# A hybrid diffusion step: late transposition in the retention, an out projection for two chunks at a time, and a paced sparse mixer

## The chip, the cores and the metric

The kernel runs on one core of a Trainium2 chip. The metric is the time of one execution on the device, in microseconds (us), as the median of several runs. The engines are TensorE (PE in the rows, and PEld for its weight loads), VectorE (DVE), ScalarE (ACT), GpSimd (POOL) and SyncE (SP), which here only issues DMA transfers. Each engine works through its own list of instructions strictly in order, so an instruction that waits holds up all that stand behind it on that engine.

## What is computed

One inference step of a two-layer trunk for two groups of tokens: a prompt of 128 tokens and a sample of 512 latent tokens, both of width 1024. Layer 0 mixes tokens by a bidirectional retention, layer 1 by windowed attention; each layer ends with a channel mixer that picks 128 of 16,384 single-neuron experts for every token (PEER). Cut to what matters here:

```python
# retention (layer 0), per head h (4 heads, key width 256, value width 512)
o  = retention(q, k, v)                     # (tokens, 512), both directions
o  = (o - mean(o)) * rsqrt(var(o) + eps)    # per token and head
y  = (silu(g) * o) @ w_out                  # 4 heads * 512 -> 1024
x  = layer_norm(alpha * x + gate * y)
# PEER (after each mixer), per token
s  = (x @ wq) . keys;  top 16 by 16, then the best 16 of each of 8 heads -> e, w
a  = gelu(sum(u[e] * x));  x = layer_norm(alpha * x + gate * sum((w * a) * v[e]))
```

## The kernel before

Tokens go in chunks of 128: one chunk of the prompt and four of the sample. PEER is done in two ways. Sample chunks 1 to 3 of each layer go the dense way (`dense`): all experts are multiplied, and a weight table of zeros and selected weights, which `scatter` makes on VectorE, GpSimd, ScalarE and TensorE (L884 to L897) and writes to device memory, masks them. The prompt and sample chunk 0 go the sparse way (`sparse`): for each of 128 slots one indirect DMA on GpSimd's queue (L817) gathers 128 rows of 2048 numbers into one of five row buffers, VectorE forms a dot product (L821), and adds the weighted second half to `acc` (L809). Two slots form a group.

In layer 0 the sample's retention runs head by head. `ret_project` makes q, k, v and the gate of a head, with matrix products of 512 columns (L325) and of 256 (L348). `ret_whole` takes a head's four chunks in turn: `pairs` makes the scores of the chunk after this one (L424) and VectorE weighs them (`att`, L427); L443 and L447 add up the chunk's output `po`; then `ret_finish` takes its mean and variance (L363, L365), multiplies by the gate into `y` (L367), starts the reciprocal root on VectorE (L178 to L180), goes on with it on ScalarE, which also scales an identity by it (`diag`, L369), and multiplies `y` by `diag` on TensorE (L372), which scales and transposes in one step; ScalarE copies the result into `yT`. `mix` interleaves one head's `ret_whole` with the projection of the next head by a fixed ratio of steps; the last head has no projection beside it.

After the retention come, per sample chunk, the out projection (`out_proj`, L228, with weights in sixteen blocks of 512 KB from device memory for each call), the layer norm (L201 to L206), the scores (L653, L658), the top-16 search on VectorE (L628 to L636) and the selection (L692 to L775, transposed by TensorE at L780). The prompt's layer-1 attention (from L495) also stands in this stage; it starts from `xp1`, the prompt after its sparse PEER of layer 0. The stage ends with the last `scatter`, and `dense` (L864) of layer 0 follows.

Program order is only a priority: a scheduler at build time puts each engine's instructions in order, and work written later is taken early where it fits. So the prompt's sparse PEER, written behind the retention (`go(sparse(0, 0, ...))`), stands in VectorE's list among the retention's own steps.

## Time and profile before

| quantity | value |
|---|---|
| median of 3 runs | 4226.44 us |
| lowest and highest run | 4223.5 and 4227.94 us |
| the profiled execution, whole | 4227.91 us |
| its span from first to last instruction | 4225.8 us |
| mean granted clock of TensorE over the span | 0.965 |

The profiled execution lies 1.5 us above the median. 2.1 us of it lie outside the span.

### The profile page before, as it was taken

The page shows a single profiled execution, that of the slowest core. Times are in us where ns is not written, and L with a number is a line of the kernel's source. Part 1 is how long each engine was busy: PE and PEld are TensorE (multiplying, and loading weights), DVE is VectorE, ACT ScalarE, POOL GpSimd, SP SyncE. Part 2 cuts the span into 40 slices and gives each one's busy share as a digit, 9 for nine tenths or more (in the row PEclk, how much of TensorE's full clock was granted, in tenths as well). Part 3 has the DMA queues.
Part 4 walks back from the last instruction along what each step waited for, and adds up shares of the span by engine and source line. Part 5 has one row for each costly group of instructions (what it writes and reads, how often), then busy time and mean ns, then how long its engine had stood idle before and what let it go on. Part 6 is the DMA issues. An engine that isn't in the chain of part 4 may idle for free.

```text
span 4225.8 us, 57107 instructions
## 1 busy us (share of the span) xinstructions
PE 3928.4 (93%) x20292; PEld 3265.7 (77%) x20292; DVE 3154.8 (75%) x6873; ACT 1675.1 (40%) x3934; POOL 1139.7 (27%) x902
## 2 busy tenths in 40 slices
PE   7998989689987999999999979899879999999996
PEld 4675666456977999999999956577669999999995
DVE  1128888825877898888898933666678989888899
ACT  2212232211664444444444433455534444444442
POOL 0002333200673222222222300334422222222232
PEclk8999999899998999999999989999989999999998
DMA  9978888788876898988888725457689889898885
GB/s 375 366 240 326 333 334 319 273 261 276 268 233 207 304 362 325 350 334 336 331 343 336 294 83 157 137 165 220 181 297 346 327 339 340 336 352 328 333 339 218
DMA packets 485453, 1227.84 MB, mean 291 GB/s; under 512 B 27568, under 2 KB 302640, under 8 KB 409392
## 3 DMA queue, kind: packets, MB, share of 16 engines
q1 hardware_dynamic: 411440, 687.30, 47.5%
q0 software_dynamic: 73728, 536.90, 32.7%
q8 instruction: 159, 2.61, 0.2%
q14 instruction: 126, 1.03, 0.1%
HBM read 1166.69 MB, written 57.41 MB: 290 GB/s over the span
## 4 chain that ended last, share of the span: by engine, by line
PE 50%; issue 7%; DVE 4%; DMA 3%; POOL 3%; ACT 1%; SPq 0%; POOLq 0%; DVEq 0%; ACTq 0%
PE bank L864 20%; PE acc L864 19%; POOL rows L817 3%; PE aside L653 2%; PE bank L495 2%; PE sc L894 2%; DMA rows<-keysT 1%; PE aside L228 1%; PE bank L609 1%; PE bank L591 1%; DMA v<-uv 1%; DMA wh<-attn_w_in 1%; DMA wo<-attn_w_out 0%; DMA rows<-uv,ei 0%; PE sc L609 0%
## 5 line engine op out<-in xcount | busy, mean ns | idle before, releaser
L817 POOL DMA_INDIRECT rows<-uv,ei x512 | 767.5, 1499 | 2235.6 <-DVE acc L809 1639.8
L864 PE MATMUL bank<-hH,uH 128*128 128x384 f32 x2048 | 697.1, 340 | 26.2 <-ACT uH L856 22.1
L864 PE MATMUL bank<-hH,uL 128*128 128x384 f32 x2048 | 696.5, 340 | 6.3 <-DVE uL L857 6.3
L864 PE MATMUL bank<-hL,uH 128*128 128x384 f32 x2048 | 696.5, 340 | 0.0
L821 DVE CUSTOM_DVE_ANT_0 rows<-rows,h 128x1024 f32<-128x1024 f32 x512 | 623.8, 1219 | 63.0 <-DMA rows<-uv,ei 62.6
L809 DVE SCALAR_TENSOR_TENSOR acc<-rows,co,acc 128x1024 f32<-128x1024 f32 x508 | 651.1, 1282 | 7.2
L864 PE MATMUL acc<-vH,cH 128*128 128x512 f32 x1536 | 599.4, 390 | 4.0 <-ACT cH L856 4.0
L864 PE MATMUL acc<-vL,cH 128*128 128x512 f32 x1536 | 598.9, 390 | 0.0
L864 PE MATMUL acc<-vH,cL 128*128 128x512 f32 x1536 | 528.2, 389 | 0.0
L856 ACT CAST uH<-u 128x1024 fp32r<-128x1024 f32 x256 | 269.6, 1053 | 582.7 <-PE bank L864 560.5
L857 DVE TENSOR_TENSOR uL<-u,uH 128x1024 fp32r<-128x1024 f32 x256 | 313.1, 1223 | 141.2 <-ACT uH L856 130.5
L864 PEld LDWEIGHTS bank<-hH,uH 128*128 128x128 f32 x2048 | 386.8, 189 | 37.2 <-ACT uH L856 22.7
L864 PEld LDWEIGHTS bank<-hL,uH 128*128 128x128 f32 x2048 | 386.5, 189 | 9.7
L864 PEld LDWEIGHTS bank<-hH,uL 128*128 128x128 f32 x2048 | 386.3, 189 | 7.6 <-DVE uL L857 7.6
L856 ACT CAST vH<-v 128x1024 fp32r<-128x1024 f32 x256 | 268.9, 1051 | 247.3 <-PE acc L864 235.3
L857 DVE TENSOR_TENSOR vL<-v,vH 128x1024 fp32r<-128x1024 f32 x256 | 312.8, 1222 | 66.9 <-ACT vH L856 65.9
L864 PEld LDWEIGHTS acc<-vH,cL 128*128 128x128 f32 x1536 | 288.3, 188 | 59.9
L864 PEld LDWEIGHTS acc<-vH,cH 128*128 128x128 f32 x1536 | 288.9, 188 | 54.9 <-ACT cH L856 4.7
L864 PEld LDWEIGHTS acc<-vL,cH 128*128 128x128 f32 x1536 | 288.9, 188 | 50.0
L348 PE MATMUL bank<-w,hT 128*128 128x256 f32 x1280 | 295.8, 389 | 26.1 <-DVE vg L353 14.6
L348 PEld LDWEIGHTS bank<-w,hT 128*128 128x128 f32 x1280 | 246.5, 195 | 80.3 <-DVE vg L353 17.1
L890 POOL TENSOR_SCALAR rows<-cst,sel 128x128 f32<-128x128 f32 x192 | 176.8, 930 | 479.3 <-ACT sel L781 324.8
(391 smaller groups left out, 5865.3 us busy)
## 6 DMA issues: line engine op xcount, KB each, us to landing
u<-ut SPq DMA_DIRECT2D x256, 512.0 KB, 7.6
v<-uv SPq DMA_DIRECT2D x256, 512.0 KB, 7.0
wh<-wq SPq DMA_DIRECT2D x160, 512.0 KB, 5.7
w<-ret_w_in SPq DMA_DIRECT2D x48, 1024.0 KB, 9.1
Wd<-stg SPq DMA_DIRECT2D x48, 1024.0 KB, 6.1
W<-Wd SPq DMA_DIRECT2D x32, 1536.0 KB, 11.5
yT<-mod_w SPq DMA_DIRECT2D x40, 1024.0 KB, 10.1
wo<-ret_w_out SPq DMA_DIRECT2D x80, 512.0 KB, 5.9
```

Of the source, the lines that this page charges most:

```text
L228: PE.matmul(acc[j], aTs[j][:, kk, :], w[:, k, :], start=(kk == 0), stop=(kk == nk - 1))
L348: PE.matmul(p[:, :256], st.hT[:, k, c * P:(c + 1) * P], w[:, k, :], start=(k == 0), stop=(k == KT - 1))
L495: PE.matmul(p[:, :256], hT[:, k, :], w[k], start=(k == 0), stop=(k == KT - 1))
L653: PE.matmul(p[:, :T], w[k][:, a * P:(a + 1) * P], hT[:, k, :], start=(k == 0), stop=(k == KT - 1))
L809: V.scalar_tensor_tensor(acc, rows[j][:, D:], co[:, j:j + 1], acc, op0=ALU.mult, op1=ALU.add)
L817: G.indirect_dma_start(out=r, out_offset=None, in_=uv[i], in_offset=bass.IndirectOffsetOnAxis(ap=ei[:, sl:sl + 1], axis=0))
L821: V.tensor_tensor_reduce(rows[j][:, :D], rows[j][:, :D], h2, 1.0, 0.0, ALU.mult, ALU.add, a[:, j:j + 1])
L856: S.copy(hi, x)
L857: splits.append(V.tensor_tensor(lo, x, hi.bitcast(F32), op=ALU.subtract))
L864: PE.matmul(out, x, y, start=start and n == 0, stop=stop and n == 2, skip_group_check=True)
L890: (G if t > 1 else V).tensor_scalar(ah[:, t, :], C["iota"], sel[:, 0, t0 + t:t0 + t + 1], sel[:, 2, t0 + t:t0 + t + 1], op0=ALU.is_equal, ...
L894: PE.matmul(p[:, t * P:(t + 1) * P], ah[:, t, :], bh[:, t, :], start=True, stop=True)
```

## The change

It has three parts.

1. `ret_finish` is split. `ret_norm` does the statistics, `y` and `diag`; `ret_turn` does the product with `diag` and the copy. In `ret_whole` a chunk's `ret_turn` now comes after the next chunk's L443 and L447. For that `y` takes a slot of `att`'s ring, which has three buffers in place of two, and `diag` has two.
2. `out` takes two chunks for one pass over the out projection's weights: first chunks 1 and 2, then chunks 3 and 0 beside the scores of chunk 1. The scores of chunks 2, 3 and 0 then all run beside the prompt's attention and the scatters; before, those of chunk 2 ran beside the fourth out projection.
3. `sparse` of the prompt in layer 0 is paced. `ret_norm` records each of its VectorE steps that make `y`. Groups 0 to 2 are free; from group 3 on, two or three groups at a time are traced within `issue_after` of the next recorded step of the sample's 16, so that their VectorE instructions stand behind it in VectorE's list; groups 40 to 63 stand behind the sixteenth.

```diff
@@ -241,6 +241,8 @@
 
 
     hident = const.tile([P, P], F32, name="hident")
+
+    paced = []
 
     def ret_consts(rc, tmp):
         V.tensor_scalar(hident, ident, 0.5, None, op0=ALU.mult)
@@ -358,15 +360,19 @@
         for st, out in zip(streams, got):
             st.heads.append((h, *out))
 
-    def ret_finish(rp, h, c, po, sg, yT):
+    def ret_norm(rp, c, po, sg, deep=1):
+
         bn = lnp.tile([P, 6], F32, name="gbn")
         V.bn_stats(bn, po)
         mv = lnp.tile([P, 2], F32, name="gmv")
         V.bn_aggr(mv, bn)
-        y = rp.tile([P, 512], F32, name="y")
-        V.scalar_tensor_tensor(y, po, mv[:, 0:1], sg[:, c, :], op0=ALU.subtract, op1=ALU.mult)
-        diag = rp.tile([P, P], F32, name="diag")
+        y = rp.tile([P, 512], F32, name="y", tag="att" if deep > 1 else "y", bufs=3 if deep > 1 else 1)
+        paced.append(V.scalar_tensor_tensor(y, po, mv[:, 0:1], sg[:, c, :], op0=ALU.subtract, op1=ALU.mult))
+        diag = rp.tile([P, P], F32, name="diag", bufs=deep)
         S.activation(diag, hident, AF.Identity, scale=rstd_of(mv[:, 1:2], scalar=True))
+        return y, diag
+
+    def ret_turn(h, c, y, diag, yT):
         p = bank()
         for j in range(4):
             PE.matmul(p[:, j * P:(j + 1) * P], y[:, j * P:(j + 1) * P], diag, start=True, stop=True)
@@ -396,7 +402,7 @@
         V.tensor_tensor(att, pa[:, :P], M[:, h, :], op=ALU.mult)
         PE.matmul(po, att, v[:, 0, :], start=True, stop=True, skip_group_check=True)
         yield
-        ret_finish(rp, h, 0, po, sg, yT)
+        ret_turn(h, 0, *ret_norm(rp, 0, po, sg), yT)
 
     def ret_whole(rp, rc, stream, yT):
 
@@ -423,11 +429,11 @@
                 for d in range(2):
                     PE.matmul(pa[:, j * P:(j + 1) * P], k_[:, d, j * P:(j + 1) * P], q[:, d, c * P:(c + 1) * P],
                               start=(d == 0), stop=(d == 1), skip_group_check=True)
-            att = rp.tile([P, 4, P], F32, name="att", bufs=2)
+            att = rp.tile([P, 4, P], F32, name="att", bufs=3)
             V.tensor_tensor(att, pa.rearrange("p (a b) -> p a b", b=P), m[:, 3 - c:7 - c, :], op=ALU.mult)
             return att
 
-        att = pairs(0)
+        att, normed = pairs(0), None
         yield
         for c in range(n):
             qs = []
@@ -447,9 +453,14 @@
                     PE.matmul(po, qs[r][:, d, :], st[r][:, d, :], start=False, stop=(r == 1 and d == 1),
                               skip_group_check=True)
                 yield
-            ret_finish(rp, h, c, po, sg, yT)
+            if normed:
+                ret_turn(h, c - 1, *normed, yT)
+            normed = ret_norm(rp, c, po, sg, 2)
             att = nxt
             yield
+        yield
+        ret_turn(h, n - 1, *normed, yT)
+        yield
 
     def mix(*gens):
 
@@ -781,6 +792,7 @@
             S.copy(dst, p[:, :384].rearrange("p (a b) -> p a b", b=P))
 
     GR = 2
+    PACE = 2.5
     CUT = 30
     MODSPAN = 120
     RES = 2
@@ -789,7 +801,7 @@
     def row_tile():
         return sp_pool.tile([P, 2 * D], F32, name="rows", bufs=ROWS)
 
-    def sparse(i, s, x, sel, y=None, cut=0):
+    def sparse(i, s, x, sel, y=None, cut=0, pace=None):
         ei, w = sel
         h2 = sp_pool.tile([P, D], F32, name="h2")
         with tc.high_priority():
@@ -809,6 +821,10 @@
                     V.scalar_tensor_tensor(acc, rows[j][:, D:], co[:, j:j + 1], acc, op0=ALU.mult, op1=ALU.add)
 
         for g in range(NSLOT // GR):
+            behind = pace[min(int(g / PACE), len(pace)) - 1] if pace and g >= PACE else None
+            es = ExitStack()
+            if behind is not None:
+                es.enter_context(tc.issue_after(behind.ins))
             rows = []
             a = sp_pool.tile([P, GR], F32, name="a", bufs=3)
             for j in range(GR):
@@ -830,6 +846,7 @@
             if prev:
                 accumulate(*prev)
             prev = (g, rows, co)
+            es.close()
             if g + 1 == cut:
                 accumulate(*prev)
                 prev = None
@@ -1112,13 +1129,13 @@
 
             def retain_sample():
                 for h in range(3):
-                    yield from mix((21, aside(ret_whole(rp, rc, sample, yT), "rec")),
+                    yield from mix((22, aside(ret_whole(rp, rc, sample, yT), "rec")),
                                    (13, ret_project(wp, rc, h, [sample])))
                 yield from aside(ret_whole(rp, rc, sample, yT), "rec")
 
             go(retain_sample())
             rcs.close()
-            go(sparse(0, 0, xp1, psel.pop()))
+            go(sparse(0, 0, xp1, psel.pop(), pace=paced[4:]))
     xpool = ctx.enter_context(tc.tile_pool(name="xs", bufs=4, reuse_waits="tile", side="right"))
     xs = [xpool.tile([P, D], F32, name="xs") for _ in range(4)]
     hd = ExitStack()
@@ -1138,8 +1155,9 @@
             late.append(peer_prompt(Packed(), wp, 1, xp1, psel))
             yield from take(8, late[0])
 
-        def out(c):
-            return out_proj(wp, 0, 1, [yT[:, :, c * P:(c + 1) * P]], 16, ret_w_out, [xs[c]], lambda j: xs[c])
+        def out(*cs):
+            return out_proj(wp, 0, 1, [yT[:, :, c * P:(c + 1) * P] for c in cs], 16, ret_w_out,
+                            [xs[c] for c in cs], lambda j: xs[cs[j]])
 
         def score(c):
             if c in X[0]:
@@ -1148,17 +1166,18 @@
 
         def spread(bp, c):
             o = X[0].index(c) * P
+            while not sl:
+                yield
             yield from aside(scatter(bp, bp, sl.pop(0), dn0[1][:, :, o:o + P, :]), "sc")
 
         order = X[0] + Y[0]
-        go(out(order[0]))
+        go(out(*order[:2]))
         s = [score(c) for c in order]
-        run((18, chain(out(order[1]), out(order[2]))), (18, s[0]))
-        run((10, out(order[3])), (18, s[1]))
+        run((10, out(*order[2:])), (18, s[0]))
         ys.close()
         with tc.tile_pool(name="bp", bufs=2, reuse_waits="tile") as bp:
             pr = prompt()
-            run((36, chain(s[2], s[3])), (40, pr), (26, chain(*(spread(bp, c) for c in X[0]))))
+            run((54, chain(*s[1:])), (40, pr), (26, chain(*(spread(bp, c) for c in X[0]))))
     dense_late(0, *dn0, pick(0, X), None)
     hd.close()
     for c in Y[0]:
```

Line numbers behind these places are 2 to 19 higher in the changed kernel: L372 becomes L378 (`ret_turn`), L424 L430, L443 L449, L447 L453, L809 L821, L821 L837, L894 L911. Three places show how the built lists of instructions differ.

TensorE's list at the end of the retention, in the last head, which has no projection beside it. `rec` are the retention's PSUM banks. Before, from the third chunk on, with the first out projection behind it:

```order
L424 MATMUL rec<-qk_2963,qk_3013 128x128 x8
L443 MATMUL rec<-vg_3085,att 128x512 x4
L447 MATMUL rec<-st_3396,qs 128x512 x2
L447 MATMUL rec<-st_3397,qs 128x512 x2
L372 MATMUL rec<-diag,y 128x128 x4
L443 MATMUL rec<-vg_3085,att 128x512 x4
L447 MATMUL rec<-st_3396,qs 128x512 x2
L447 MATMUL rec<-st_3397,qs 128x512 x2
L372 MATMUL rec<-diag,y 128x128 x4
L228 MATMUL bank<-wo,yT 128x512 x6
```

After, the same stretch:

```order
L430 MATMUL rec<-qk_2963,qk_3013 128x128 x8
L449 MATMUL rec<-vg_3084,att 128x512 x4
L453 MATMUL rec<-st_3396,qs 128x512 x2
L453 MATMUL rec<-st_3397,qs 128x512 x2
L378 MATMUL rec<-diag,y 128x128 x4
L449 MATMUL rec<-vg_3084,att 128x512 x4
L453 MATMUL rec<-st_3396,qs 128x512 x2
L453 MATMUL rec<-st_3397,qs 128x512 x2
L378 MATMUL rec<-diag,y 128x128 x8
```

Before, each product with `diag` stands directly behind the L447 whose result it is made from. After, the product of a chunk stands behind the next chunk's products, and the last two stand together ahead of the out projection.

VectorE's list at the end of the retention: the last `y`, with the start of its reciprocal root, up to the out projection's first step (L236). `acc<-rows` and `rows,a<-rows` are the prompt's sparse slots. Before:

```order
L363 BN_STATS gbn<-rec 128x6
L365 BN_AGGR gmv<-gbn 128x2
L367 SCALAR_TENSOR_TENSOR y<-rec,gmv,vg_3230 128x512
L178 TENSOR_SCALAR rs_3601<-gmv 128x1
L179 TENSOR_SCALAR rs_3602<-rs_3601 128x1
L180 TENSOR_SCALAR rs_3602<-rs_3602 128x1
L236 TENSOR_TENSOR bank<-bank,gb 128x512
L237 SCALAR_TENSOR_TENSOR xs<-xs,bank 128x512
```

After, the start of the same stretch (six more dot products and eight more accumulations follow ahead of L236):

```order
L368 BN_AGGR gmv<-gbn 128x2
L837 ISA rows,a<-rows,h_3624 128x1024
L837 ISA a 128x1
L821 SCALAR_TENSOR_TENSOR acc<-rows,co,acc 128x1024
L370 SCALAR_TENSOR_TENSOR y<-rec,gmv,vg_3224 128x512
L178 TENSOR_SCALAR rs_3601<-gmv 128x1
L837 ISA rows,a<-rows,h_3624 128x1024
L837 ISA a 128x1
L843 TENSOR_TENSOR a<-a,wsp 128x2
L179 TENSOR_SCALAR rs_3602<-rs_3601 128x1
L845 SCALAR_TENSOR_TENSOR co<-th,a 128x2
L180 TENSOR_SCALAR rs_3602<-rs_3602 128x1
```

Before, all 128 slots of the prompt stand ahead of this place. After, 78 stand ahead of the last `y` and 50 behind it, all of those ahead of VectorE's first step of the scatter.

TensorE's list at the end of the stage, up to the first matmul of `dense` (L864 before, L881 after). `sc` are the scatter's banks, `bank<-rows` the prompt's scores. Before:

```order
L658 MATMUL bank<-rows 128x128
L653 MATMUL bank<-rows,wh 128x128 x8
L894 MATMUL sc<-bh,ah 128x128 x3
L658 MATMUL bank<-rows 128x128
L894 MATMUL sc<-bh,ah 128x128 x4
L658 MATMUL bank<-rows 128x128
L894 MATMUL sc<-bh,ah 128x128 x64
L864 MATMUL bank<-hH,uH 128x384
```

After:

```order
L664 MATMUL bank<-rows,wh 128x128 x3
L911 MATMUL sc<-bh,ah 128x128 x8
L664 MATMUL bank<-rows,wh 128x128 x8
L669 MATMUL bank<-rows 128x128
L911 MATMUL sc<-bh,ah 128x128 x8
L669 MATMUL bank<-rows 128x128
L911 MATMUL sc<-bh,ah 128x128 x104
L881 MATMUL bank<-hH,uH 128x384
```

The run of scatter matmuls with nothing beside them, at the very end, grows from 64 to 104.

## Rows read from the trace of the kernel before

**Rows 1.** The page: busy us (share of the span) and instructions of each engine.

```profile
PE 3928.4 (93%) x20292; PEld 3265.7 (77%) x20292; DVE 3154.8 (75%) x6873; ACT 1675.1 (40%) x3934; POOL 1139.7 (27%) x902
```

**Rows 2.** Busy time by stage, 358 to 1351 us from the start; columns in the first row.

```profile
core 0: us, PE busy (x) PEld busy (x) DVE busy (x) ACT busy (x) POOL busy (x), PEclk, DMA share, GB/s
358.00:865.00 507.00, 428.10 (x1604) 292.40 (x1605) 409.18 (x733) 140.53 (x508) 169.04 (x125) 0.92 0.84 311
865.00:1063.00 198.00, 186.40 (x866) 118.41 (x866) 87.68 (x399) 33.70 (x92) 7.31 (x8) 0.97 0.87 282
1063.00:1120.00 57.00, 54.29 (x396) 51.16 (x395) 52.41 (x234) 31.44 (x84) 35.54 (x36) 1.00 0.95 294
1120.00:1224.00 104.00, 96.93 (x735) 84.38 (x735) 86.59 (x381) 80.65 (x235) 84.38 (x86) 1.00 0.65 191
1224.00:1341.00 117.00, 102.12 (x786) 95.96 (x784) 90.03 (x428) 58.78 (x156) 64.32 (x64) 0.92 0.71 216
1341.00:1351.00 10.00, 0.75 (x2) 0.50 (x2) 0.79 (x2) 1.04 (x1) 0.00 (x0) 0.50 0.93 261
```

**Rows 3.** TensorE's waits, 400 to 870 us: us in total, times, longest us.

```profile
PE rec L372 <- ACT diag L369: 59.0, 11, 11.2
PE bank L348 <- DVE vg L353: 14.6, 2, 7.5
PE bank L348 <- DVE qk L331: 3.8, 1, 3.8
```

**Rows 4.** TensorE in order of time, 402 to 432 us: start, us, instruction.

```profile
402.96 1.95 PE L424 MATMUL rec<-qk,qk 128*128 128x128 f32 x16
404.75 3.60 PE L443 MATMUL rec<-vg,att 128*128 128x512 f32 x8
408.18 3.60 PE L447 MATMUL rec<-st,qs 128*128 128x512 f32 x8
422.96 2.08 PE L372 MATMUL rec<-diag,y 128*128 128x128 f32 x8 [11.18 <-ACT diag L369]
424.83 3.46 PE L424 MATMUL rec<-qk,qk 128*128 128x128 f32 x16
```

**Rows 5.** VectorE in order of time ahead of the product at 422.96 us.

```profile
413.28 0.69 DVE L363 BATCH_NORM_STATS2 gbn<-rec 128x6 f32<-128x512 f32 x1
...
416.71 1.19 DVE L821 CUSTOM_DVE_ANT_0 rows<-rows,h 128x1024 f32<-128x1024 f32 x1
...
417.83 0.74 DVE L367 SCALAR_TENSOR_TENSOR y<-rec,gmv,vg 128x512 f32<-128x512 f32 x1
...
418.86 0.15 DVE L180 TENSOR_SCALAR rs<-rs 128x1 int32<-128x1 int32 x1
```

**Rows 6.** VectorE's groups, 343 to 1400 us: times | busy us, mean ns | idle before.

```profile
L809 DVE SCALAR_TENSOR_TENSOR acc<-rows,co,acc 128x1024 f32<-128x1024 f32 x127 | 162.9, 1283 | 1.9
L821 DVE CUSTOM_DVE_ANT_0 rows<-rows,h 128x1024 f32<-128x1024 f32 x128 | 156.0, 1220 | 54.4 <-DMA rows<-uv,ei 54.2
L890 DVE TENSOR_SCALAR ah<-cst,sel 128x128 f32<-128x128 f32 x192 | 60.6, 356 | 9.3 <-PE sc L894 4.7 <-ACT sel L781 4.6
```

**Rows 7.** TensorE in the first out projection, in order of time.

```profile
881.35 15.62 PE L228 MATMUL bank<-wo,yT 128*128 128x512 f32 x36
```

**Rows 8.** The page's DMA queues (packets, MB, share) and issues (KB, us to landing).

```profile
q0 software_dynamic: 73728, 536.90, 32.7%
...
wo<-ret_w_out SPq DMA_DIRECT2D x80, 512.0 KB, 5.9
```

**Rows 9.** Busy time in 50 us of the retention, columns as in group 2.

```profile
450.00:500.00 50.00, 49.31 (x217) 40.19 (x217) 39.03 (x66) 16.32 (x59) 18.75 (x15) 1.00 0.98 374
```

**Rows 10.** Busy time in the scatter's last stretch, columns as in group 2.

```profile
1308.00:1341.00 33.00, 22.70 (x136) 19.66 (x135) 32.66 (x121) 20.76 (x50) 29.98 (x28) 0.82 0.45 128
```

**Rows 11.** TensorE in order of time at the start of the dense pass.

```profile
1350.25 0.69 PE L864 MATMUL bank<-hH,uH 128*128 128x384 f32 x1 [10.02 <-ACT uH L856]
```

## The prediction, made before the changed kernel had run

> **What bounds the kernel now.** I read the page first. TensorE is busy for 93% of the span and VectorE for 75% [rows 1]; ScalarE and GpSimd have room. So what a change is worth depends on the stage, and on whether TensorE waits there.
>
> The lists of instructions of before and after agree from the start of `dense` on, but for neighbours that change places. The stage to cost therefore runs from 358 us (the first L424 of the sample's retention) to 1351 us (the first L864). I cut it at five marks that both kernels have: the first out projection (865 us), the first scatter matmul (1063), the last transposition of the second dense chunk's selection (1120), that of the third chunk's (1224), the last scatter matmul (1341) [rows 2].
>
> The table by stage shows where time is lost. In the retention TensorE is busy for 428 of 507 us, at a mean granted clock of 0.92, while VectorE is busy for 409. In the next 198 us TensorE is busy for 186 and VectorE for only 88. That is the room to which the change moves work. From 1063 us both are busy for most of the time.
>
> The waits say what TensorE lacks in the retention: 59.0 us for `diag` in 11 waits, 14.6 and 3.8 for VectorE's steps on the projections [rows 3]. The timeline shows one such wait: after 11.18 us the eight rows of the product take 2.08 us and the sixteen rows of L424 3.46, where the same sixteen took 1.95 before [rows 4]. The granted clock has fallen to its lower level, so a wait costs more than its length.
>
> VectorE's timeline shows why `diag` is late. The statistics (L363) begin at 413.28, `y` at 417.83, L180 ends at 419.0, with sparse steps of 1.2 us between them; ScalarE then needs until 422.96 for its ten small steps [rows 4, 5]. VectorE is not full. It has the sparse slots standing ahead.
>
> **Unit costs.** In TensorE's list a float32 matmul counts once, in the trace twice. Four of 512 columns take 3.43 us (404.75 to 408.18), so 0.86 each; eight of 128 take 1.79, so 0.224 [rows 4]; 256 columns I put at half of 0.86. Thirty-six trace rows of the out projection in 15.62 us agree with 0.86 [rows 7]. A sparse slot costs VectorE 1.22 for L821 and 1.28 for L809 [rows 6], 2.5 us together.
>
> **The retention.** By these costs its matmuls need 401 us: three head projections of 32 at 512 columns and 128 at 256 (248 us), and four heads of 48 at 128 columns and 32 at 512 (153 us). The other 106 of the 507 us are 79 of waits and 27 of slow clock and small gaps. After the change a product with `diag` has the next chunk's L443 and L447 ahead of it, 7 us at least, and in the first three heads pieces of a projection too. The chain from L447 to `diag` is 5.6 us without sparse steps in it (1.6 on VectorE, 4 on ScalarE) and 8 to 11 with two to four of them. So in the first three heads I count nothing; the projections cover it, and without that cover it would be the 59 us again.
>
> What stays: in the last head VectorE's list from the first to the fourth `y` holds 37 us of work (12 slots among it) while TensorE's holds 26, so some 11 us; the last two products have no cover but each other, 10 us; the waits for the projections' VectorE steps fall from 18 to perhaps 4, since VectorE now has 271 us of work in this stage for 409; slow clock and gaps 12. That is 401 + 37 = 438 us, 69 less than 507. Bounds: 420 (only the last wait and some slow clock stay) and 460 (half of the 59 us comes back).
>
> **From the first out projection to the first scatter matmul.** TensorE needs 182 us for either order; the second pass over the weights saves 16 transposes of `gb`, 3.6 us over the whole stage, and 32 loads of 512 KB, 16.8 MB [rows 8]. The point is VectorE. Its list now holds 50 sparse slots here, 125 us, and 95 us of the rest (the 88 of [rows 2] without the scatter's first 5, and 12 for four more rows of the search and the second layer norm). Of these 220 us some 4 are done when TensorE begins, but the order fixes where VectorE then stands: it does six slots, and waits for the first half of both chunks' products (28 us in, some 14 idle), again for the second half (10 idle), and a little for the scores' inputs (4). That is 244 us. Everything after the first layer norm (from some 78 us in) is then a VectorE list of 160 us beside 117 us of TensorE work.
>
> Gathers and weights meet there. Between the starts of the first and the second chunk's scores VectorE's list is 95 us, and 24 gathers of 1.05 MB (536.9 MB for 512, [rows 8]), 16 blocks of `wq` and 14 to 16 of the out projection, some 42 MB, belong in it. The best stretch of the retention moved 374 GB/s [rows 9], which makes 112 us. Weights loaded ahead (11 buffers, 5.8 MB) and row buffers soften it; I take half of the 17 us and 4 for what I miss: 256 us, 58 more than before. Bounds: 243 and 276.
>
> **The rest of the stage.** Before, TensorE's lists between the next marks need 57, 97 and 92 us, and took 57, 104 and 117 [rows 2]. After, they need 47, 118 and 79.
>
> First scatter to second selection: the prompt's layer norm is 28 us of VectorE behind the scatter's first step, and the prompt's first products, the keys, values and queries (30 us) wait for it: 28 + 30 + 5 for the chain between them, 63 us. Before, `xp1` was long ready here.
>
> To the third selection: 118 at the ratio of before (104 to 97), less a little since the attention now stands beside two chunks' scores, 124 us.
>
> The end: VectorE's list from the third selection holds 101 us, TensorE's 79. In the last 33 us of before VectorE was busy for 32.7 [rows 10], so it is what limits the scatter; now all 32 steps of the third chunk's scatter stand behind the scores. 101 and some gaps: 108 us, 9 less than before. The 10.02 us until the first L864 stay [rows 11].
>
> **Sum.** 438 + 256 + 63 + 124 + 108 = 989 us where before has 507 + 198 + 57 + 104 + 117 = 983. The retention gives back 69 us, the three parts behind it take 84, the end gives 9. That is 6 us longer: 4233.9 for the profiled execution's 4227.91, and 4232 against the median of 4226.44. A measurement here tells 0.2% (8.5 us) from nothing; this is inside it.
>
> **Rivals.**
>
> *VectorE keeps up and the kernel is faster.* The retention comes to 422 us and the stretch behind it to 245, with no loss to the DMA queues; the rest as above less 2: 422 + 245 + 293 = 960, 23 us less than 983, 4203. For it speaks that TensorE's waits shrink together with the slow clock that follows them; against it that VectorE's 220 us behind the retention stand in a fixed order. It decides where the first out projection begins: before about 785 us it is this one.
>
> *Gathers hold up weights, and weights gathers.* Then the 17 us stand in full, not half, and TensorE waits for blocks of weights as well, which I put at 12: some 20 us on top, 4252. For it: 42 MB in 95 us is 440 GB/s, and no stretch of the profile moved that. The Trainium skill says on the page DMA: Bandwidth & Descriptors, section Specifications, that device memory gives a core about 358 GB/s. By that figure the 42 MB would take an estimated 117 us instead of 112; the 374 GB/s of [rows 9] are above it, so the trace doesn't bear it out as a limit.
>
> *The wait in the retention only moves.* `att` for the next chunk and `y` share a ring of three now, and VectorE is the longer list in the last head. If half of the 59 us reappears at L443 or at the later product, the retention takes 468 and the kernel 4262.
>
> **How the numbers follow.** The balance as summed: 0.47, with 4215 to 4248 as its own range from the bounds of the retention and the stretch behind it. Faster by VectorE: 0.29. The queues: 0.15. The moved wait: 0.09. The range 4200 to 4263 takes in the faster case and both slower ones. Faster by over 0.2%: 0.27 of the first rival and 0.06 of the balance, 0.33. Slower: 0.22 from the two others and 0.17 of the balance, 0.39. The same: 0.28.
>
> **What the profile of after would show.** Right: waits of L378 for `diag` of 15 us or less in all; the first out projection near 796 us; VectorE busy for over 85% between it and the first scatter matmul, and that matmul near 1052; TensorE waiting there for VectorE and for blocks of weights by some 50 us; the first matmul of `dense` near 1357. Wrong: an out projection that starts after 815, a first scatter matmul less than 235 us behind it, or a difference that arises behind the start of `dense`, where I see no cause.

## The result, and the profile after

The changed kernel takes 4252.46 us (4248.72 to 4256.44), the kernel before, measured beside it, 4225.19 us. The ratio is 1.0064, with a 95% interval of 1.0047 to 1.0081: slower by 20 to 34 us. The forecast was 4232 us, from 4200 to 4263. So the time lies inside the range, but above the 4215 to 4248 of the likeliest case; it is the time that I had given to the rival with the queues.

The profiled execution is the longest of the four, 4256.44 us, 28.5 longer than that of before. The page of the kernel after shows the same engines with the same work [rows 1]:

```profile
span 4254.7 us, 56960 instructions
PE 3948.0 (93%) x20276; PEld 3280.3 (77%) x20276; DVE 3156.0 (74%) x6861; ACT 1671.3 (39%) x3930; POOL 1120.3 (26%) x902
```

What moved is seen by stage. This is the busy time of the kernel after in the stages of [rows 2], with the same columns: the retention, the stretch from the first out projection to the first scatter matmul, the parts up to the second and the third selection, the end, and the gap ahead of `dense`.

```profile
359.10:810.50 451.40, 413.29 (x1601) 282.48 (x1601) 277.59 (x520) 117.73 (x411) 98.01 (x79) 0.95 0.64 237
810.50:1078.60 268.10, 212.36 (x867) 140.50 (x868) 217.58 (x618) 51.02 (x178) 66.36 (x51) 0.86 0.91 335
1078.60:1134.20 55.60, 49.90 (x304) 43.83 (x303) 50.88 (x190) 35.99 (x92) 45.73 (x45) 0.97 0.67 205
1134.20:1255.40 121.20, 117.48 (x894) 102.70 (x893) 94.18 (x420) 84.22 (x245) 76.69 (x80) 1.00 0.81 248
1255.40:1363.50 108.10, 93.20 (x704) 86.83 (x702) 84.26 (x413) 54.12 (x142) 62.88 (x64) 0.92 0.55 165
1363.50:1372.60 9.10, 0.00 (x0) 0.00 (x0) 0.02 (x1) 1.63 (x2) 0.00 (x0) 0.59 0.82 241
```

The retention gives back 55 us. The stretch behind it takes 268 us, 74 more than before. (My mark for the first scatter matmul of before, 1063, is late by 3.6: one group of eight stands at 1059.4. So before, the stretch took 194 us and the part behind it 60; from here on I use these.) The first matmul of `dense` comes at 1372.6 us, 22 later than before. The other 6.5 us arise behind it, in the part whose lists are the same.

TensorE's waits between 400 and 815 us in the kernel after (us in total, times, longest), beside [rows 3]: 

```profile
PE rec L378 <- ACT diag L372: 21.9, 4, 12.4
PE bank L350 <- DVE vg L355: 15.5, 3, 6.2
```

The late transposition does what it says: of 59.0 us for `diag` 21.9 are left, all but 1.7 of them in the last head. The waits for the projections' VectorE steps have hardly changed: 15.5 us, where [rows 3] has 14.6 and 3.8. And these are TensorE's waits in the stretch behind the retention, where before it waited for 10 us in all:

```profile
PE aside L669 <- DMA kk<-keysT: 25.9, 6, 7.3
PE aside L664 <- ACT s L672: 8.2, 3, 5.3
PE aside L664 <- DMA wh<-wq: 8.1, 3, 3.0
PE aside L169 <- DVE xs L206: 4.4, 1, 4.4
```

The scores' key blocks (`kk`, 128 KB each) come late, and blocks of `wq`. VectorE waits in the same stretch:

```profile
DVE a L843 <- ACT th L842: 16.1, 12, 3.7
DVE bank L236 <- PE bank L228: 14.5, 2, 9.1
DVE sv L639 <- ACT s L672: 10.5, 5, 3.1
DVE rows L837 <- DMA rows<-uv,ei: 6.0, 8, 2.3
```

Two engines in one loop: 217.6 us of work and the 47.1 of waits shown here are 265 of the stretch's 268 us on VectorE. One link of the loop in order of time, from the timelines of TensorE, ScalarE and VectorE (start, us, instruction):

```profile
927.11 1.19 PE L669 MATMUL aside<-kk,pq 128*128 128x128 f32 x4 [5.97 <-DMA kk<-keysT]
928.34 0.37 ACT L672 COPY s<-aside 128x256 f32<-128x256 f32 x1 [6.58 <-PE aside L669]
928.75 0.49 DVE L639 MAX8 sv<-s 128x8 f32<-128x128 f32 x2 [3.08 <-ACT s L672]
```

A key block is late, TensorE waits for it, ScalarE for TensorE, VectorE for ScalarE, and behind VectorE's top-16 step stand the next sparse slots and the second half of the layer norm's input. The stretch itself has two limits. Three stretches of 10 us of the kernel after, columns as in [rows 2]:

```profile
950.00:960.00 10.00, 10.00 (x46) 6.17 (x45) 9.14 (x28) 1.39 (x6) 2.80 (x2) 1.00 1.03 415
990.00:1000.00 10.00, 2.24 (x7) 1.40 (x7) 9.72 (x25) 0.91 (x3) 2.80 (x2) 0.65 1.11 359
1020.00:1030.00 10.00, 8.73 (x50) 8.57 (x51) 10.00 (x41) 2.08 (x8) 1.89 (x3) 0.64 0.85 278
```

Up to 1000 us the DMA engines are full for most of the time, at up to 415 GB/s; from 1000 to 1060 VectorE is busy without a gap, and TensorE, at a lower granted clock, has to wait for it.

### The profile page after: what moved, and what is told of

Same layout as the page of the kernel before. It is cut to its first block, busy times and chain, and to the rows that moved or that the text cites. A ratio compares the mean times of both kernels' runs of the same rounds, so it can differ in the third digit from the quotient of the medians.

```text
span 4254.7 us, 56960 instructions
## 1 busy us (share of the span) xinstructions
PE 3948.0 (93%) x20276; PEld 3280.3 (77%) x20276; DVE 3156.0 (74%) x6861; ACT 1671.3 (39%) x3930; POOL 1120.3 (26%) x902
## 4 chain that ended last, share of the span: by engine, by line
PE 60%; DMA 4%; DVE 3%; ACT 1%; issue 0%; POOL 0%; SPq 0%; ACTq 0%; DVEq 0%
PE bank L881 25%; PE acc L881 24%; PE aside L664 3%; PE bank L506 2%; PE sc L911 2%; DMA wh<-attn_w_in 1%; PE bank L620 1%; PE aside L228 1%; PE bank L602 1%; DMA rows<-keysT 1%; DMA v<-uv 1%; DMA wo<-attn_w_out 1%; PE bank L615 0%; DMA Wd<-stg 0%; PE sc L620 0%; PE aside L669 0%
## 5 line engine op out<-in xcount | busy, mean ns | idle before, releaser
L833 POOL DMA_INDIRECT rows<-uv,ei x512 | 751.4, 1468 | 2478.0 <-DVE acc L821 1855.1
L881 PE MATMUL bank<-hH,uH 128*128 128x384 f32 x2048 | 697.3, 340 | 31.1 <-ACT uH L873 24.1
L881 PE MATMUL bank<-hH,uL 128*128 128x384 f32 x2048 | 696.3, 340 | 4.0 <-DVE uL L874 4.0
L881 PE MATMUL bank<-hL,uH 128*128 128x384 f32 x2048 | 696.4, 340 | 0.0
L821 DVE SCALAR_TENSOR_TENSOR acc<-rows,co,acc 128x1024 f32<-128x1024 f32 x508 | 651.7, 1283 | 6.7
L837 DVE CUSTOM_DVE_ANT_0 rows<-rows,h 128x1024 f32<-128x1024 f32 x512 | 624.1, 1221 | 43.7 <-DMA rows<-uv,ei 43.5
L881 PE MATMUL acc<-vH,cH 128*128 128x512 f32 x1536 | 599.1, 390 | 4.0 <-ACT cH L873 4.0
L881 PE MATMUL acc<-vL,cH 128*128 128x512 f32 x1536 | 598.6, 390 | 0.0
L881 PE MATMUL acc<-vH,cL 128*128 128x512 f32 x1536 | 521.7, 389 | 0.0
L881 PEld LDWEIGHTS bank<-hH,uH 128*128 128x128 f32 x2048 | 386.7, 189 | 41.7 <-ACT uH L873 24.4
L881 PEld LDWEIGHTS bank<-hL,uH 128*128 128x128 f32 x2048 | 386.5, 189 | 9.8
L881 PEld LDWEIGHTS bank<-hH,uL 128*128 128x128 f32 x2048 | 386.3, 189 | 5.5 <-DVE uL L874 5.5
L881 PEld LDWEIGHTS acc<-vH,cL 128*128 128x128 f32 x1536 | 288.3, 188 | 60.0
L881 PEld LDWEIGHTS acc<-vH,cH 128*128 128x128 f32 x1536 | 289.0, 188 | 54.8 <-ACT cH L873 4.7
L881 PEld LDWEIGHTS acc<-vL,cH 128*128 128x128 f32 x1536 | 288.9, 188 | 50.0
L350 PE MATMUL bank<-w,hT 128*128 128x256 f32 x1280 | 295.9, 389 | 23.8 <-DVE vg L355 15.5
```

Source lines behind the costliest of these rows:

```text
L350: PE.matmul(p[:, :256], st.hT[:, k, c * P:(c + 1) * P], w[:, k, :], start=(k == 0), stop=(k == KT - 1))
L821: V.scalar_tensor_tensor(acc, rows[j][:, D:], co[:, j:j + 1], acc, op0=ALU.mult, op1=ALU.add)
L833: G.indirect_dma_start(out=r, out_offset=None, in_=uv[i], in_offset=bass.IndirectOffsetOnAxis(ap=ei[:, sl:sl + 1], axis=0))
L837: V.tensor_tensor_reduce(rows[j][:, :D], rows[j][:, :D], h2, 1.0, 0.0, ALU.mult, ALU.add, a[:, j:j + 1])
L881: PE.matmul(out, x, y, start=start and n == 0, stop=stop and n == 2, skip_group_check=True)
```

## The experiments

Two theories at the start. By the **queue theory** the loss behind the retention is transfers: the gathers of the late slots take DMA time from the key blocks and weights. By the **list theory** it is VectorE's list, in which the late slots stand ahead of what TensorE needs. Behind both stands the question which of the three parts does what.

All runs, with the ratio to the kernel before measured on the same chip. The stages are the retention, the stretch to the first scatter matmul, and from there to the last scatter matmul, in the profiled execution; "both" is the sum of stretch and scatter; "slots behind" is the number of the 128 dot products that stand behind the last `y` in VectorE's list. The first scatter matmul doesn't stand behind the same work in every kernel's list, so two stretches compare only roughly; the last one does, so "both" compares.

| kernel | median us | ratio (95%) | retention | stretch | scatter | both | slots behind |
|---|---|---|---|---|---|---|---|
| before | 4225.2 to 4219.2 | 1 | 507 | 194 | 280 | 474 | 0 |
| after | 4252.5 | 1.0064 (1.0047 to 1.0081) | 451 | 268 | 285 | 553 | 50 |
| no_pace | 4188.3 | 0.9911 (0.9893 to 0.9928) | 474 | 199 | 276 | 474 | 5 |
| no_late | 4307.6 | 1.0189 (1.0171 to 1.0208) | 512 | 272 | 273 | 546 | 48 |
| one_out | 4251.4 | 1.0069 (1.0053 to 1.0086) | 450 | 290 | 271 | 561 | 50 |
| still_rows | 4202.8 | 0.9951 (0.9935 to 0.9968) | 455 | 233 | 277 | 510 | 50 |
| small_slots | 4232.3 | 1.0029 (1.0018 to 1.0040) | 453 | 240 | 295 | 535 | 50 |
| pace40 | 4185.6 | 0.9918 (0.9899 to 0.9936) | 455 | 201 | 278 | 479 | 15 |
| late_only | 4187.8 | 0.9924 (0.9906 to 0.9942) | 470 | 190 | 283 | 473 | 5 |
| two_out_only | 4227.7 | 1.0021 (1.0010 to 1.0032) | 508 | 202 | 276 | 478 | 0 |
| pace32 | 4190.9 | 0.9927 (0.9910 to 0.9945) | 447 | 219 | 275 | 494 | 32 |
| late_pace40 | 4186.7 | 0.9920 (0.9903 to 0.9937) | 455 | 214 | 272 | 486 | 15 |
| pace_only | 4294.3 | 1.0183 (1.0162 to 1.0205) | 512 | 285 | 265 | 550 | 48 |
| two_key_buffers | 4262.4 | 1.0099 (1.0081 to 1.0117) | 451 | 251 | 323 | 574 | 50 |

**Without pacing (no_pace).**

```diff
-            go(sparse(0, 0, xp1, psel.pop(), pace=paced[4:]))
+            go(sparse(0, 0, xp1, psel.pop()))
```

> The changed kernel with its slots unpaced again (late transposition and the out projection for two chunks stay), so all 128 slots stand in the retention. Queue theory (the loss behind the retention is transfers: 45 gathers among the weights) and list theory (it is VectorE's list) agree here that the stretch behind the retention falls from 268 us to about 195 (198 before the change). They leave open what the late transposition does when VectorE is full: if it covers the waits for diag, as the 59 us of before suggest, the retention takes about 455 us and the kernel about 4180; if VectorE's slots make every step of a chunk late, so that the wait only moves to the next chunk's att or to the later product, the retention stays at 490 or more and the kernel at 4210 or more.

The stretch is at 199 us, as both theories said, and the kernel 0.9% faster than before: the late transposition covers its waits with VectorE full as well. In the retention 474 us lies between the two guesses; 26.8 us of waits for the product's inputs are left, and 24.4 for `vg`.

**Without the late transposition (no_late).**

```diff
-            if normed:
-                ret_turn(h, c - 1, *normed, yT)
-            normed = ret_norm(rp, c, po, sg, 2)
+            ret_turn(h, c, *ret_norm(rp, c, po, sg, 2), yT)
```

> The changed kernel with the transposition back directly behind the L453 of its own chunk (paced slots and the out projection for two chunks stay). If the late transposition is what frees TensorE, the wait for diag comes back with the bare chain of 5.6 us at most of the sixteen products, 25 to 45 us more than the 21.9 us measured, and the kernel takes 4275 to 4295. If thinning VectorE's list is enough, the retention takes within 8 us of the 451 us measured and the kernel 4245 to 4260.

4308, above the first answer, and a retention of 512 us, as long as before the change, although VectorE is busy for 289 us of it in place of 409. TensorE's wait for `diag` in it:

```profile
PE rec L378 <- ACT diag L372: 67.7, 8, 11.5
```

Thinning VectorE's list in this way, with the slots right behind each `y`, gives the retention nothing by itself.

**Out projection for one chunk at a time (one_out).** The calls of before are put back: `go(out(order[0]))`, then `chain(out(order[1]), out(order[2]))` beside the first scores, `out(order[3])` beside the second.

> The changed kernel with the out projection for one chunk at a time (32 more loads of 512 KB, 16.8 MB) and the scores beside it as in the kernel before. Queue theory: the stretch behind the retention moves 16.8 MB more at some 400 GB/s, 25 to 40 us longer, 4275 to 4290. List theory: VectorE's list is the same length and its first layer norm comes earlier, so 4240 to 4255.

Half each: the stretch grows by 22 us, and TensorE now waits for 34.6 us for blocks of the out projection (0.8 in the kernel after), as the queue theory said; but the next part gives 14 of them back, and the time, 4251, is that of the list theory.

**Without the last 48 gathers (still_rows).**

```diff
+            still = pace and g >= 40
+            rows = list(prev[1]) if still else []
...
-            for j in range(GR):
+            for j in range(0 if still else GR):
...
-                V.tensor_tensor_reduce(rows[j][:, :D], rows[j][:, :D], h2, ...)
+                V.tensor_tensor_reduce(rows[j][:, :D], rows[j][:, D:] if still else rows[j][:, :D], h2, ...)
```

> The changed kernel without the last 48 gathers of the prompt's layer 0 (50 MB): groups 40 to 63 work on the rows that group 39 gathered, with all of their VectorE and ScalarE steps, so that part of the mixer's sum is left out. Queue theory: the waits for key blocks and weights behind the retention (34 us) go, with the slow clock beside them; the stretch takes 225 to 240 us in place of 268, and the kernel 4210 to 4225. List theory: VectorE's 218 us of work set the stretch, which stays at 255 or more, and the kernel at 4240 or more.

The stretch takes 233 us, the queue theory's number, and the kernel 4203, 7 us below its 4210. In the stretch, columns as in [rows 2], and then TensorE's longest waits there:

```profile
812.20:1045.40 233.20, 201.54 (x860) 128.14 (x861) 202.91 (x575) 53.13 (x180) 8.42 (x8) 0.92 0.54 176
```

```profile
PE aside L169 <- DVE xs L206: 20.0, 1, 20.0
PE bank L228 <- DMA wo<-ret_w_out: 4.4, 2, 3.9
```

The waits for key blocks are gone, the DMA share falls to 0.54, and what is left is VectorE: busy for 87%, and a 20 us wait of the scores for the layer norm that stands behind slots. So the queues are not all of it, and the list theory has a part. But the run changes more than the transfers: of the 50 slots behind the last `y`, 48 have their dot product ahead of the first layer norm's last step here (L206, at 921 us), and 15 in the kernel after (881 us). The 20 us wait belongs to this order, which is not that of the kernel after.

**Small slots (small_slots).** Dot product and accumulation of groups 40 to 63 over 8 columns: `[:, :n]` with `n = 8 if short and g >= 40 else D`.

> The changed kernel with all of its gathers, but with the dot products and accumulations of groups 40 to 63 over 8 of 1024 columns (part of the mixer's sum is left out), so that VectorE has some 110 us less to do behind the retention and the queues as much as before. Without those gathers the stretch fell by 35 us, from 268 to 233, and 39 us above the kernel before stayed. If those 39 us are VectorE's list, and the two add up, the stretch takes 225 to 240 us here and the kernel 4205 to 4225. If the queues' 90 MB set it alone, it stays above 250 and the kernel above 4235. If the gathers only hurt because VectorE's list is full, it falls to 200 to 215 and the kernel to 4185 to 4200.

With VectorE at 112 us in place of 218 the stretch takes 240 us, and now the DMA engines are full in it. The stretch, and the part from there to the last scatter matmul:

```profile
811.60:1051.80 240.20, 195.28 (x795) 122.21 (x795) 112.49 (x569) 49.34 (x171) 46.25 (x49) 0.90 0.97 362
1051.80:1346.90 295.10, 268.10 (x1969) 245.03 (x1968) 231.21 (x1073) 176.67 (x486) 186.30 (x190) 0.95 0.69 211
```

TensorE waits for key blocks for 19.0 us and for blocks of the out projection for 7.2. But the 240 us hold less work than the 268: 795 rows of matmuls stand ahead of the first scatter matmul here, 867 in the kernel after, and the missing 72 (64 of the scores' L664 and 8 of L669) fall into the next part, which takes 10 us more. So the stretch meets the expectation and the time, 4232, is above it. The stretches of still_rows and no_pace, in turn, have 90 rows of the prompt's first products in layer 1 (L506) in them, which that of the kernel after hasn't.

From the first out projection to the last scatter matmul, with the same work in all four, no_pace takes 474 us, still_rows 510, small_slots 535 and the kernel after 553. So the late slots' VectorE work without transfers costs 36 us, the transfers with little VectorE work 61, and both together 79. Both theories hold, and their losses overlap. In these two runs the transfers weigh more: without them 43 us go, without the VectorE work 18 (the ratio falls from 1.0064 to 0.9951 and to 1.0029). The exact shares stay open, because still_rows has an order of its own. When the last of the 128 dot products starts (last start in each line) says the same; still_rows, then small_slots:

```profile
L838 DVE CUSTOM_DVE_ANT_0 rows<-rows,h x128: 1207/1216/1227, 357.6 to 926.0; 128x1024 f32<-128x1024 f32 x128
L841 DVE CUSTOM_DVE_ANT_0 rows<-rows,h x128: 114/1217/1226, 358.3 to 1031.5; 128x1024 f32<-128x1024 f32 x80, 128x8 f32<-128x8 f32 x48
```

In the kernel after it starts at 1054.

**More of the slots ahead of the last y (pace40, pace32).** `PACE = 2.5` becomes 4.0 and 3.2.

> The changed kernel with four groups for each recorded step in place of two and a half (PACE = 4.0), so that all but four slots stand ahead of the last y, evenly. If the place of the last 48 slots is the whole loss, the stretch behind the retention takes 195 to 205 us and the kernel 4180 to 4195, as without pacing. If even spacing also helps the retention beyond leaving it to the scheduler (474 us), it is at 465 or less and the kernel at 4165 to 4180.

> The changed kernel with PACE = 3.2: 96 slots stand ahead of the last y and 32 behind it, between the 78 and 50 of PACE = 2.5 (4252 us) and the 113 and 15 of PACE = 4.0 (4186 us). If every slot behind the retention costs the same, about 35 slots for 66 us, this takes 4215 to 4225. If VectorE and the queues have room there for some slots and the loss begins only past it (VectorE was idle for 110 us of the 194 before the change), it takes 4185 to 4200.

pace40: the stretch 201 and the retention 455, both as expected, and the time no better than no_pace: the part from `dense` on took 2887 us in its profiled execution against 2871. pace32: the second answer. 32 slots behind the retention cost the kernel nothing that can be measured (0.9927, where 15 give 0.9918): behind the retention they take 15 us more (494 and 479), and the retention gives 8 of them back. 18 more cost 59 us there and some 60 in the time. Two timelines show what lies between. From the kernels pace32 and then after, VectorE's dot products from 799 us on and the prompt's first products in layer 1 (L506; ns, then first and last start):

```profile
L837 DVE CUSTOM_DVE_ANT_0 rows<-rows,h x32: 1205/1217/1226, 799.1 to 947.5; 128x1024 f32<-128x1024 f32 x32
L506 PE MATMUL bank<-wh,rows x96: 378/379/483, 978.4 to 1034.5; 128*128 128x256 f32 x96
```

```profile
L837 DVE CUSTOM_DVE_ANT_0 rows<-rows,h x51: 1200/1219/1470, 799.5 to 1054.0; 128x1024 f32<-128x1024 f32 x51
L506 PE MATMUL bank<-wh,rows x96: 379/379/382, 1108.8 to 1132.0; 128*128 128x256 f32 x96
```

In pace32 the last dot product starts at 948 us, and the prompt's attention at 978, much as without pacing (985). In the kernel after, the slots lie on until 1054, among top-16 steps that wait for late key blocks, and the prompt's attention starts at 1109. That its late start makes the loss is read from these lines; no run moves it alone.

**One part alone (late_only, two_out_only, pace_only).** late_only is the kernel after with the edits of no_pace and one_out; two_out_only puts the calls of `out` for two chunks into the kernel before; pace_only adds `paced`, `PACE = 2.5` and the `issue_after` to the kernel before.

> The kernel before with the late transposition alone (with the deeper rings and the 22 to 13 steps that go with it): slots unpaced, out projection for one chunk at a time. If the late transposition is the whole gain of the unpaced kernel, 4185 to 4200. If the out projection for two chunks gives much of the 35 us, above 4205.

> The kernel before with the out projection for two chunks alone, slots unpaced and the transposition where it was. The waits for its blocks were 6.4 us before and 16 transposes go (3.6 us): 4213 to 4225 against 4223. If the later first layer norm and the missing cover of the scores' chains cost more than that, 4226 to 4240.

> The kernel before with pacing alone (PACE = 2.5). The changed kernel without the late transposition took 512 us for the retention although VectorE was busy for only 289 of them, so thinning VectorE's list doesn't shorten the wait for diag by itself. If that holds with the out projection for one chunk too, the retention takes 500 to 515, the stretch behind it 265 to 290, and the kernel 4290 to 4315. If the chain to diag does get shorter by it, the retention is at 485 or less and the kernel below 4280.

late_only came at 4188, the first answer, two_out_only at 4228, the second, and pace_only at 4294 with a retention of 512, the first. With no_pace, one_out and no_late these make all combinations of the three parts. The late transposition gives 0.8 to 1.2% in every one of them (0.9924 alone; 0.9911 for 1.0021, 1.0069 for 1.0183, 1.0064 for 1.0189). Pacing at 2.5 costs 1.5 to 1.8% in every one. The out projection for two chunks changes the ratio by at most 0.2%. Why pacing doesn't shorten the wait for `diag` is seen in VectorE's timeline of pace_only, in the last head:

```profile
836.50 0.75 DVE L369 SCALAR_TENSOR_TENSOR y<-rec,gmv,vg 128x512 f32<-128x512 f32 x1
837.16 0.14 DVE L178 TENSOR_SCALAR rs<-gmv 128x1 f32<-128x1 f32 x1
837.22 1.22 DVE L828 CUSTOM_DVE_ANT_0 rows<-rows,h 128x1024 f32<-128x1024 f32 x1
...
841.85 0.15 DVE L179 TENSOR_SCALAR rs<-rs 128x1 int32<-128x1 int32 x1
...
843.18 0.15 DVE L180 TENSOR_SCALAR rs<-rs 128x1 int32<-128x1 int32 x1
```

The slots are queued behind `y`, and so ahead of L179 and L180, which `diag` needs: three dot products and two accumulations, 6 us, stand in the chain. The product at 846.76 waits for 11.51 us, longer than any of [rows 3]. The products ahead of it and behind it wait for 11.51 and 11.25.

**Both good parts (late_pace40).** The late transposition, `PACE = 4.0`, the out projection for one chunk.

> The late transposition with PACE = 4.0 and the out projection for one chunk at a time. With paced slots the retention took 455 us against 470 unpaced, and the out projection for one chunk made the stretch behind it 190 us against 199 to 201. If both hold together, 455 + 192 and some 4172 to 4182, less than any kernel so far. If the 15 slots that now stand behind the retention collide with the 32 loads more, as the 50 did (34.6 us of waits for blocks of the out projection), 4186 to 4200.

The second answer: 15 slots and 32 loads more collide again (19.8 us of waits for blocks of the out projection), and the kernel is as fast as late_only.

**Two key buffers (two_key_buffers).** `kk` gets `bufs=max(2, deep)`.

> The changed kernel with two buffers for the sample's key blocks (kk) in place of one, so that a block's load can be issued one pass of the scores earlier. If the 25.9 us of waits for kk come from the single buffer, they fall below 8 us and the kernel to 4225 to 4240. If the bytes are the limit, the wait moves to the blocks of wq and of the out projection, and the kernel stays at 4245 to 4258.

Neither. The waits for `kk` fall to 3.6 us and the stretch to 251, which speaks for the single buffer as what turns full queues into these waits, though a wait of 21.3 us at L151, for ScalarE, is new in the stretch. But the built lists came out differently: the last slots now stand behind the first scatter steps, the prompt's attention starts at 1135 us, and the scatter part takes 323 us. So the time doesn't tell what the buffer is worth.

## Why the prediction was right and where it failed

**Unit costs and the retention.** 438 us were forecast, 451 measured, of the bounds 420 and 460. The matmuls' 401, the 21 us for `diag` (21.9, of which 20.2 in the last head) and 12 for slow clock and gaps (TensorE's busy time of 413 is 12 above the 401) came as summed. The term that was off is the wait for the projections' VectorE steps: 4 put, 15.5 measured, as large as before. My reason, that VectorE has less to do there, doesn't decide it.

**Why diag was late.** I wrote that VectorE is not full but has the sparse slots standing ahead. The slots do stand in the chain, but pacing moves slots to just that place, as pace_only shows, and alone it leaves the retention at 512 us. It is the late transposition that takes the wait off the path: 37 us alone, 60 beside the paced slots. What pacing adds to it in the retention is 23 us at PACE = 2.5, and 19 at 4.0.

**The last head.** Here even the late product waited for 12.40 us. ScalarE had done eight of ten steps by 797.4 us; from VectorE's, ScalarE's and TensorE's timelines of the kernel after:

```profile
799.51 1.23 DVE L837 CUSTOM_DVE_ANT_0 rows<-rows,h 128x1024 f32<-128x1024 f32 x1 [3.42 <-DMA rows<-uv,ei]
800.78 0.20 ACT L839 ACTIVATE th<-a 128x2 f32<-128x2 f32 x1 [3.35 <-DVE a L837]
800.89 0.28 ACT L185 ACTIVATE rs<-rs,rs 128x1 f32<-128x1 f32 x1
801.70 2.08 PE L378 MATMUL rec<-diag,y 128*128 128x128 f32 x8 [12.40 <-ACT diag L372]
```

A slot's step (L839) stands in ScalarE's list ahead of the ninth; it waits for the slot's dot product, and that for its gather. The 12.40 us are partly a transfer, which the line of the wait doesn't name.

**The stretch behind.** 256 forecast, 268 measured, 243 and 276 the bounds. VectorE's work was right (220 us forecast, 217.6 measured), and its waits for the out projection were put too high (24 forecast, 14.5 measured). Missing was the loop: 16.1 us for ScalarE's `th`, for which the sum has no term but the 4 for what I miss, and 10.5 for the scores, for which it has 4. Half of the queues' 17 us was too little: the DMA engines are full for most of 190 us, and TensorE waits for 34 us for blocks. I had named that as a rival, at 0.15, with the same 4252 us. It was right about the place and the mechanism; that its time is the measured one is luck, since it puts 20 us on the stretch alone, and the stretch is 12 us above the sum, with the rest of the difference elsewhere. And the late slots' VectorE work, which I had in the sum, has its part in the loss.

**The rest.** 63, 124 and 108 us were forecast; 56, 121 and 108 came. 6.5 us arose behind the start of `dense`, where the lists are the same and I saw no cause. From the first matmul of `dense` to the end the profiled executions of these kernels took 2861 to 2887 us; I have not settled what sets that.

So 13 us in the retention, 12 in the stretch, 10 back behind it and 6.5 at the end make 22 of the 22.5 us by which the profiled execution is longer than its forecast of 4233.9. The errors have both signs, and it is the width of the range, 63 us, that took the time in; the likeliest case's own range missed it. The signs that I gave are mixed too: 21.9 us for `diag` in place of 15 or less, VectorE busy for 81% of the stretch in place of over 85%, and the difference behind the start of `dense`, which I had listed as a sign of being wrong. The direction was undecided in the forecast (0.39 slower, 0.28 the same, 0.33 faster). What decides it, as the runs show, is how many slots are moved: with 32 the same three parts gain 0.7%.

## What to carry to other kernels

Before work is moved into an engine's idle time, add up what it brings along on the other queues, and look for the consumer that waits for the last piece: here 32 slots leave its start where it was (978 us against 985), and 50 move it to 1109. An order that puts filler behind the first step of a chain puts the filler inside the chain; whether a mark at the chain's last step does better, no run here tried. Parts of one change are to be timed alone: here the late transposition gives 0.8 to 1.2%, pacing at this rate takes 1.5 to 1.8%, and the out projection for two chunks gives nothing; late_only has the whole gain with the least code, and no kernel here is measurably better.

## What was not expected of the hardware

With gathers and weight blocks together the DMA engines of the kernel after moved 393 GB/s over 50 us (950 to 1000 us), where the best 50 us of before showed 374 [rows 9]. Over 10 us they moved up to 415, and in the kernel before up to 409 (460 to 470 us), so the peak is not new, only how long it lasts. The Trainium skill gives about 358 GB/s for device memory and one core (DMA: Bandwidth & Descriptors, Specifications); the trace is above it here too, so that figure is no limit for this run. In the stretch behind the retention TensorE's busy time rose from 184 to 212 us for nearly the same matmuls (852 and 867 instructions), at a mean granted clock of 0.86 in place of 0.97: the 56 us of waits there come with 28 us more of busy time, half as much again.
